# A hybrid decoder block: in-place stick-breaking scans, joint head transfers, and four more gates as a unit of seven products

## The chip, the cores and the metric

The kernel runs on one core of one Trainium2 chip. The metric is the device time of one launch in microseconds (us). TensorE (PE in the profile) does the matrix products, VectorE (DVE) and ScalarE (ACT) the elementwise work, GpSimd (POOL) and SyncE (SP) mostly issue DMA transfers, and POOL builds a mask now and then.

## The reference, cut to what matters

All is float32; there are 1024 tokens of width 1024, 256 memory tokens, 8 stick-breaking heads and 8 forgetting heads of 64, and 4 memory heads of 128. `w_in` projects the normed tokens to all queries, keys, values and to 3 x 1024 gate logits.

```python
def stick_breaking_attention(q, k, v):
    # A[t,s] = beta[t,s] * prod_{s<j<t}(1-beta[t,j]), strictly causal
    ...
        z = einsum('bhtd,bhsd->bhts', q, k) * scale
        strict = s_idx < t_idx
        log_rem = where(strict, log_sigmoid(-z), 0.0)
        after = cumsum(log_rem, axis=3, reverse=True) - log_rem
        w = where(strict, exp(log_sigmoid(z) + after), 0.0)
        out = einsum('bhts,bhsd->bhtd', w, v)
...
h = rmsnorm(x); proj = h @ w_in
o_sb  = stick_breaking_attention(sb_q, sb_k, sb_v)
o_fox = forgetting_attention(rmsnorm(fx_q), rmsnorm(fx_k), fx_v, log_f)   # causal softmax
o_mem = memory_attention(rmsnorm(m_q), rmsnorm(m_k), m_v)                 # softmax over 256
gates = sigmoid(gate_logit.reshape(b, s, 3, 1024))
merged = gates[0]*(o_sb @ w_branch_sb) + gates[1]*(o_fox @ w_branch_fox) + gates[2]*(o_mem @ w_branch_mem)
x = x + merged @ w_out
x = x + relu(rmsnorm(x) @ w_ff_up)**2 @ w_ff_down
```

## The kernel before, in words

**Precision.** A product of float32 matrices is three passes: both operands are split into a rounded part and the rest, and the passes are high by high, high by low, low by high (`passes`, `split` at L1052: ACT rounds at L1054, DVE subtracts at L1055).

**Units of seven products.** A matrix product whose two sides are cut into 2 x 2 blocks can be made from seven block products in place of eight (the kinds P1 to P7, in the order `KINDS`, L1354). `unit_products` (L1416, its matmuls are recorded on L1456) does so for the projections in `PROJ`: stick-breaking keys and queries, memory queries, forgetting keys and queries, stick-breaking values, and then the gate units of `GATES`, four gates of 128 columns each: `ga` holds gates 16 to 19, `gb` 20 to 23, `gc` 0 to 3. POOL brings the four weight blocks of a unit (L1373), DVE makes sums of them and `split` rounds them (`unit_prep`, L1379), PE multiplies, and DVE and ACT add up and evict (`unit_evict`, L1490; `unit_final`, L1519). These units run one after the other ahead of the attention. In it there are 24 gates: 0 to 7 belong to the stick-breaking branch, 8 to 15 to the forgetting branch, 16 to 23 to the memory branch.

**Dense gates.** Gates 4 to 7 and 10 to 13 are made by `dense_T` (L1147), one gate at a time: 8 steps of the contraction, 2 halves of 512 tokens, 3 passes, so 48 matmuls recorded on L1144. Gates 14 and 15 go together in `dense_two` (L1163), gate 9 comes earlier and gate 8 with the values. A gate's result goes through ACT into a row tile and by SP to `gate_scr` in device memory (`gate_put`, L1631). The three branch products follow in the order memory, stick-breaking, forgetting. The first two are `dense_branch(0)` and `dense_branch(1)` (L1728), 192 matmuls each, also on L1144; the last is `last_branch` (L1871), written out after the attention.

**Order.** The part up to `last_branch` is scheduled by a small planner at build time (`Machine`, L185 to 282). Each piece of work is a generator that asks for an engine (`Op`, with a cost from hand-written formulas), for a buffer (`Get`), or waits for an event. The planner plays this through with its own clock and emits the instructions in the order in which it began them. Gates and branch products are marked `side=True`: on PE they are chosen only when no attention operation is ready, so they fill the holes of the attention. `branches[0]` may begin only when all earlier dense tasks have been taken, `branches[1]` when `branches[0]` has been. Transfers are generators with a planned cost of their own (`transfer`, L296).

**Stick-breaking attention.** There are four pairs of heads `sb` and then four pairs `fox` (L809). For a head and 128 query rows, `sb_tile` (L812) goes over chunks of up to 512 keys, the last chunk first in the scan. The queries carry a sign such that `Sigmoid(+scale * sc)` is 1 - beta and `Sigmoid(-scale * sc)` is beta. Per chunk: two score matmuls (L823, L824); in the chunk that holds the diagonal, DVE adds a mask block of large numbers to PSUM (L834), so that 1 - beta is 1 and beta is 0 there; two ACT sigmoids, one into a tile `rho` taken from `RQ` (L827), one into the row tile `beta` (L828); and one DVE scan from right to left (L843) that leaves 1 - (what is left of the stick) in `beta`: `out = rho * out_before + beta`. `RQ` holds four 512-wide halves of two of the three row tiles of `RR`; `whole_again` (L1626) gives these two back after the four stick-breaking pairs. With the remaining one the memory attention works meanwhile (`RR`).

`unit` (L888) takes two such row tiles, transposes blocks of them on PE (L917), splits each turned block into a rounded part (ACT, L922) and the rest (DVE, L924), multiplies by the values (L934), and evicts. Since the row tile holds sums rather than weights, the values are differences of neighbouring rows (`value_step`, L1568).

**Loads of the heads.** `load_pairs` (L984) brings each head's operands from device memory by DMAs that POOL issues (`put`, L1004). `p_scr` holds for each projection two tensors, rounded part and rest. For each half of 512 tokens, `k1` is the rounded keys twice (lower and upper 64 partitions), `k2` the rest of the keys (twice for `sb`), `q` the rounded queries over the rest. That is 12 DMAs for a stick-breaking head, 16 for a forgetting head.

**Memory attention** (`memory`, L573, outputs at L701) runs within the stick-breaking stage, and its outputs are what `dense_branch(0)` multiplies. The forgetting attention (`fox_tile`, L854, scores on L869) follows, then the rest of the second branch, `last_branch`, the output projection (L1981) and the MLP (L2658).

Of the kernel before, what the change touches and what calls it, by code (L numbers as in the profile page):

```python
# [21 lines left out]
P = 128  # L22
# [5 lines left out]
HD = 64  # L28
# [15 lines left out]
def tile_hybrid_block(  # L44
# [58 lines left out]
    sm = C.p.tile([P, 8], F32, tag="sm", name="sm")  # L103
    zero, one = sm[:, 0:1], sm[:, 1:2]
    nc.vector.memset(zero, 0.0)
    nc.vector.memset(one, 1.0)
    gq2, gk2, gmq, gmk, bfg, eps = (sm[:, i:i + 1] for i in range(2, 8))
    nc.vector.memset(eps, EPS * 2.0 ** (2 / 3))

    def root_table():  # L110
# [8 lines left out]
    p_scr = {k: [dram.tile([512, S], F32, name=f"{k}_scr{i}", tag=f"{k}_scr{i}") for i in range(2)]  # L119
             for k in ("sbq", "sbk", "fxq", "fxk", "mq")}  # L120
# [230 lines left out]
    ES, OO, EL, RR, HT, PH, PL, OB, VV, BK, LATER, NONE, RQ = (Places([]) for _ in range(13))  # L351
# [221 lines left out]
    def memory():  # L573
        yield pairs[0].over

        def fetched_q(h, half):
            q = yield Get(HT, 2)

            def issue():
                for t, scr in zip(q, p_scr["mq"]):  # L580
                    nc.gpsimd.dma_start(f32(t), scr[h * P:(h + 1) * P, half * 512:(half + 1) * 512])
            yield from transfer(issue, 2 * P * 512 * 4, 1.1, queue_="POOL")
            q_of[h, half] = q
        q_of = {}
        for c in range(2):
            yield in_scr["mq", c]
            kv = yield Get(HT, 4)

            def issue():
                for i, t in enumerate(kv):  # L590
                    nc.gpsimd.dma_start(f32(t), m_scr[c][:, i, :])
            loaded = spawn(transfer(issue, 4 * P * 512 * 4, 2.2, queue_="POOL"), -20.0)
            evs = []
            for h in (2 * c, 2 * c + 1):
                for half in range(2):
                    ev = spawn(fetched_q(h, half), -300.0)
                    yield ev
                    yield loaded
                    if len(evs) > 1:
                        yield evs[-2]  # L600
                    evs.append(spawn(mem_attention(h, half, kv, q_of[h, half]), -10.0))
            if c:
                machine.fire(mem_in)
            for ev in evs:
                yield ev
            HT.put(*kv)
        machine.fire(mem_over)
# [204 lines left out]
    def sb_tile(pair, b, i, beta):  # L812
# [5 lines left out]
        def chunk(ci, c, m, u):  # L818
            rho = yield Get(RQ)
            sc = yield Get(SC)  # L820

            def scores():
                nc.tensor.matmul(sc[:, :m], q, pair.t["k1", b, ci][:, :m], start=True, stop=False)  # L823
                nc.tensor.matmul(sc[:, :m], q, pair.t["k2", b, ci][:, :m], start=False, stop=True)  # L824

            def sigmoids():
                nc.scalar.activation(rho[:, :u], sc[:, :u], AF.Sigmoid, scale=HD ** -0.5)  # L827
                nc.scalar.activation(beta[:, c:c + u], sc[:, :u], AF.Sigmoid, scale=-HD ** -0.5)  # L828
# [59 lines left out]
    def unit(pair, b, g, es):  # L888
# [5 lines left out]
        scr, r0 = o_scr[0 if pair.kind == "sb" else 1], (2 * pair.p + b) * HD  # L894
# [5 lines left out]
        def block(k):  # L900
# [11 lines left out]
            def turn():  # L912
# [71 lines left out]
    def load_pairs():  # L984
        yield ready
        for c, pair in enumerate(pairs):
# [5 lines left out]
            for b in range(2):  # L992
# [4 lines left out]
                def halves(half):  # L997
# [7 lines left out]
                    lower, upper, f4 = slice(0, HD), slice(HD, P), slice(HD, HD + 4)  # L1005

                    def keys():
                        put("k1", lower, ks_[0][rows, cols])
                        put("k1", upper, ks_[0][rows, cols])
                        put("k2", lower, ks_[1][rows, cols])  # L1010
                        if fox:
                            put("k2", f4, fk_scr[2 * p + b, :, cols])
                        else:
                            put("k2", upper, ks_[1][rows, cols])

                    def queries():
                        put("q", lower, qs[0][rows, cols])
                        put("q", upper, qs[1][rows, cols])
                        if fox:
                            put("q2", lower, qs[0][rows, cols])  # L1020
# [3 lines left out]
                evs = [spawn(transfer(k0_, 4 * HD * 2048, 1.6, queue_="POOL"), -20.0), spawn(transfer(k1_, 4 * HD * 2048, 1.6, queue_="POOL"), -20.0),  # L1024
                       spawn(transfer(q1_, (3 if fox else 2) * HD * 2048, 1.2, queue_="POOL"), -20.0),
                       spawn(transfer(q0_, (3 if fox else 2) * HD * 2048, 1.2, queue_="POOL"), -20.0)]
# [328 lines left out]
    GATES = {"ga": 16, "gb": 20, "gc": 0}  # L1355
# [163 lines left out]
    def unit_final(u, ct, q, src, of_bank=False):  # L1519
# [14 lines left out]
        elif u in ("sbq", "sbk"):  # L1534
# [10 lines left out]
            def out_():  # L1545
                for scr, t_ in zip(p_scr[u], (hi, lo)):
                    nc.sync.dma_start(scr[rows, cols], t_)
            spawn(counted(u, c, spawn(stored(out_, hi, lo))))
        else:
# [5 lines left out]
            def out_(hi, lo):  # L1555
                for scr, t_ in zip(p_scr[u], (hi, lo)):
# [4 lines left out]
    def masked(t):  # L1561
        nc.gpsimd.memset(t, 0.0)
        nc.gpsimd.affine_select(out=t[:, 384:], in_=t[:, 384:], pattern=[[-1, P + 1]], compare_op=ALU.is_ge,
                                fill=-NEG, base=0, channel_multiplier=1)
# [32 lines left out]
    def second_part():  # L1597
        def opened(name, *tags):
            pool = holder[name] = Pool(name, **{tag: n for _, tag, n, _, _ in tags})
            for place, tag, n, shape, dt in tags:  # L1600
# [6 lines left out]
               (LATER, "later", 1, 513, F32))  # L1607
        later = holder["later"] = LATER.free[0]
# [17 lines left out]
    def whole_again(tiles_):  # L1626
        for pair in pairs[:4]:
            yield pair.over
        RR.put(*tiles_)
# [1091 lines left out]
```

## Time and profile before

| | before |
|---|---|
| median of 3 runs | 1686.24 us (1685.2 to 1687.55) |
| span of the profiled execution | 1686.7 us |
| instructions in it | 25003 |
| DMA traffic | 284.32 MB, mean 169 GB/s |

The page of the profile has, in this order: the busy time of each engine with its share of the span and the count of instructions; the span in 40 equal slices; the DMA queues; the chain of work that ended last; the costliest groups of instructions; and the DMA issues. Two lines of the slices give the picture. Each digit is the busy share of a slice in tenths, 9 being 90% or more, and a slice is 42.2 us:

```profile
PE   9999999999999999999999999999999999999999
...
PEclk9999999999999999999999999999999999999999
```

In the lists of groups, "L1144 PE MATMUL sc<-h,whi 128x512" is the instruction that is recorded on line 1144, writing tile `sc` from the tiles `h` and `whi`; behind the bar stand the busy time and the mean time of one in ns, and then the idle time of the engine just ahead of them with what ended it. PEld is the loading of weights into PE, which overlaps its matmuls. Windows are given in us from the start of the span.

### The profile page before, as it was taken

To read this page: it belongs to the slowest core of one execution; us is meant where nothing else is said; L and a number is where in the kernel's file an instruction comes from. 1 tells how busy PE (TensorE), PEld (TensorE's weight loads), DVE (VectorE), ACT (ScalarE), POOL (GpSimd) and SP (SyncE) were. 2 spreads that over 40 slices of the span, in tenths; PEclk is the share of its full clock that TensorE was granted. 3 is DMA by queue.
4 is the path that set the end of the run, shared out by engine and by line. 5 is a ranking of instruction groups with operands and counts; after the bars stand their busy time and mean duration, and the time that the engine had idled before them with its cause. 6 is when DMAs were issued, how large, how long until landed. Compare 5 with 4: busy or idle time off the path is not lost.

```text
span 1686.7 us, 25003 instructions
## 1 busy us (share of the span) xinstructions
PE 1675.3 (99%) x9118; PEld 1432.0 (85%) x9118; DVE 1293.0 (77%) x2079; ACT 848.9 (50%) x1474; POOL 255.2 (15%) x440
## 2 busy tenths in 40 slices
PE   9999999999999999999999999999999999999999
PEld 9998899998888888888888887878888887888887
DVE  7977778855459888867877898987777776688775
ACT  6455555534358888866761446433333344332331
POOL 0000000000253151254400011022111120000000
PEclk9999999999999999999999999999999999999999
DMA  7445434467475365387747542144444484564532
GB/s 245 157 150 182 149 119 150 146 194 243 127 232 161 111 186 151 117 240 224 236 146 245 183 162 100 57 162 155 152 150 137 150 307 171 202 202 143 198 125 75
DMA packets 142221, 284.32 MB, mean 169 GB/s; under 512 B 16913, under 2 KB 53329, under 8 KB 142098
## 3 DMA queue, kind: packets, MB, share of 16 engines
q1 hardware_dynamic: 110562, 183.08, 32.0%
q0 software_dynamic: 31536, 99.64, 19.5%
q8 instruction: 72, 1.18, 0.3%
q14 instruction: 51, 0.42, 0.1%
HBM read 189.83 MB, written 92.83 MB: 168 GB/s over the span
## 4 chain that ended last, share of the span: by engine, by line
PE 92%; DVE 5%; DMA 2%; ACT 1%; issue 1%; SPq 0%; DVEq 0%; ACTq 0%
PE pp L1456 11%; PE pp L1144 10%; PE pp L1981 10%; PE pp L2658 8%; PE sc L1456 7%; PE sc L1144 6%; PE sc L1981 5%; PE sc L2658 4%; PE tr L2658 4%; PE tr L917 4%; PE pv L1456 3%; PE pv L2658 3%; PE tr L1981 2%; PE sc L934 2%; PE pp L934 2%; DVE h L1917 1%
## 5 line engine op out<-in xcount | busy, mean ns | idle before, releaser
L1055 DVE TENSOR_TENSOR wlo<-raw,whi 128x1024 fp32r<-128x1024 f32 (+1 forms) x88 | 107.5, 1222 | 80.2 <-ACT whi L1054 80.0
L1054 ACT ACTIVATE whi<-raw 128x1024 fp32r<-128x1024 f32 (+1 forms) x88 | 93.2, 1059 | 78.8 <-PE pp L1456 32.7
L2658 PE MATMUL pp<-h,sop 128*128 128x512 f32 x540 | 128.4, 396 | 0.0
L2658 PEld LDWEIGHTS pp<-h,sop 128*128 128x128 f32 x540 | 101.6, 188 | 24.4
L1981 PE MATMUL pp<-h,oh 128*128 128x512 f32 x384 | 121.1, 397 | 0.7 <-ACT cu L2066 0.6
L924 DVE TENSOR_TENSOR ptl<-tr,pth 128x512 fp32r<-128x512 f32 (+1 forms) x160 | 99.1, 628 | 24.1 <-ACT pth L922 23.1
L922 ACT ACTIVATE pth<-tr 128x512 fp32r<-128x512 f32 (+1 forms) x160 | 87.4, 556 | 36.0 <-PE sc L934 15.8
L1981 PEld LDWEIGHTS pp<-h,oh 128*128 128x128 f32 x384 | 72.0, 188 | 19.0 <-ACT cu L2066 1.4
L2573 ACT ACTIVATE h<-t 128x2048 fp32r<-128x2048 f32 (+1 forms) x17 | 30.7, 1814 | 110.2 <-DVE t L1917 97.4
L1373 POOL DMA_DIRECT2D raw<-w_in x32 | 24.2, 755 | 395.1 <-DVE wlo L1055 395.1
L1144 PE MATMUL sc<-h,whi 128*128 128x512 f32 (+1 forms) x254 | 77.7, 389 | 0.0
L1456 PE MATMUL pp<-h,whi 128*128 128x512 f32 x248 | 77.5, 394 | 0.0
L1981 PE MATMUL pp<-h,ol 128*128 128x512 f32 x192 | 76.1, 396 | 0.0
L1456 PE MATMUL pp<-whi,h 128*128 128x256 f32 x384 | 71.8, 283 | 0.0
L843 DVE TENSOR_TENSOR_SCAN e<-r,e 128x384 f32<-128x384 f32 (+3 forms) x64 | 66.3, 1044 | 6.9 <-ACT e L828 6.5
L1974 ACT ACTIVATE oh<-raw 128x512 fp32r<-128x512 f32 x64 | 39.4, 625 | 61.8 <-DVE raw L1917 61.8
L2658 PE MATMUL sc<-h,sop 128*128 128x512 f32 x264 | 63.7, 396 | 0.0
L2658 PE MATMUL tr<-h,sop 128*128 128x512 f32 x264 | 63.4, 396 | 0.0
L1917 DVE TENSOR_TENSOR sop<-ur,sop 128x2048 fp32r<-128x2048 f32 (+1 forms) x28 | 61.8, 2211 | 2.0 <-ACT sop L2586 2.0
L917 PE MATMUL tr<-ident,e 128*128 128x128 f32 x416 | 62.7, 273 | 0.0
L1456 PEld LDWEIGHTS pp<-whi,h 128*128 128x128 f32 x384 | 60.2, 188 | 0.0
L2658 PEld LDWEIGHTS sc<-h,sop 128*128 128x128 f32 x264 | 49.6, 188 | 12.3 <-DVE sop L1917 0.5
(558 smaller groups left out, 5087.7 us busy)
## 6 DMA issues: line engine op xcount, KB each, us to landing
ur<-s_scr SPq DMA_DIRECT2D x26, 1024.0 KB
raw<-w_in POOLq DMA_DIRECT2D x42, 512.0 KB, 4.9
raw<-w_up SPq DMA_DIRECT2D x60, 256.0 KB
s_scr<-s POOLq DMA_DIRECT2D x60, 256.0 KB, 2.7
g<-w_down SPq DMA_DIRECT2D x14, 1024.0 KB
s_scr<-cu POOLq DMA_DIRECT2D x48, 256.0 KB, 2.8
h<-sbk_scr POOLq DMA_DIRECT2D x64, 128.0 KB, 3.2
o<-gate_scr SPq DMA_DIRECT2D x32, 256.0 KB
```

The lines of the kernel that those rows point to most:

```text
L843: nc.vector.tensor_tensor_scan(out=back, data0=rho[:, :u][:, ::-1], data1=back, initial=0.0 if last else beta[:, c + u:c + u + 1], op0=ALU ...
L917: nc.tensor.transpose(tr[:, jj * 256 + a * P:jj * 256 + (a + 1) * P], es[a][:, j * P:(j + 1) * P], ident)
L922: yield Op("ACT", act_time(512 - lo_c), lambda: nc.scalar.activation(ph[:, lo_c:], tr[:, lo_c:], AF.Copy))
L924: yield Op("DVE", dve_time(512 - lo_c), lambda: nc.vector.tensor_tensor(pl[:, lo_c:], tr[:, lo_c:], f32(ph[:, lo_c:]), ALU.subtract))
L934: nc.tensor.matmul(pv[0][:, c_:256], pair.v[:, j, b, :], p_[:, jj * 256 + c_:(jj + 1) * 256], start=(k == 0 and n_ == 0 and i == 0), stop= ...
L1054: yield Op("ACT", 0.03 + act_time(m), lambda: nc.scalar.activation(hi, raw, AF.Copy))
L1055: yield Op("DVE", dve_time(m), lambda: nc.vector.tensor_tensor(lo, raw, f32(hi), ALU.subtract))
L1144: nc.tensor.matmul(ps, a_, b_, start=(first and i == 0), stop=(last and i == n - 1))
L1456: nc.tensor.matmul(out_, a_, b_, start=(first and n == 0 and j == 0), stop=(last and n == 3 and j == len(todo) - 1), skip_group_check=True)
L1917: nc.vector.tensor_tensor(out_, a_, b_, op)
L1981: nc.tensor.matmul(ps, w[a_][:, k * P:(k + 1) * P], h[b_][k], start=(first and k == 0 and i == 0), stop=(last and k == 3 and i == 2), skip ...
L2658: nc.tensor.matmul(ps, a_[:, c, qs], b_[:, c, :], start=(kind in ("P1", "P2", "P7") and c == 0 and i == 0), stop=(kind in ("P2", "P4", "P3 ...
```

## The change

It has four parts.

1. **What is left, in place.** `sb_tile` makes one sigmoid, 1 - beta, into the row tile and scans it in place: `out = max(in * out_before, floor)`, beginning with 1. In the chunk with the diagonal, `floor` is a tile that holds 1.0 on the masked places and 0 elsewhere, so that the masked part stays at 1; in the other chunks it is a broadcast zero. The row tile then holds what is left of the stick, and the eviction of a turned block subtracts 1 (a bias of -1 in ACT's copy, a -1 in DVE's subtraction). The sign of the value differences is turned. The addition of the mask to PSUM, the second sigmoid and the `RQ` tiles go. The floor takes half of one lent row tile, so that one tile of `RR` is lent and not two.
2. **Joint transfers.** `p_scr` becomes one tensor with a leading 2. `k1`, and `k2` of the stick-breaking heads, come by one DMA whose source is broadcast twice; `q` by one DMA over both parts. A stick-breaking head takes 6 DMAs, a forgetting head 12. The planner's costs for issuing them are changed to match.
3. **Gates 4 to 7** become a fourth gate unit `gd`, made after `gc` and ahead of the attention; the list of dense gates leaves them out by itself.
4. The mask `later` of the forgetting attention is 512 wide and not 513; it and `floor` are made by `masked` with a fill and a base.

```diff
+    sm = C.p.tile([P, 9], F32, tag="sm", name="sm")
+    zero, one, minus = sm[:, 0:1], sm[:, 1:2], sm[:, 8:9]
...
-    p_scr = {k: [dram.tile([512, S], F32, name=f"{k}_scr{i}", tag=f"{k}_scr{i}") for i in range(2)]
+    p_scr = {k: dram.tile([2, 512, S], F32, name=f"{k}_scr", tag=f"{k}_scr") for k in ("sbq", "sbk", "fxq", "fxk", "mq")}
...
-    def sb_tile(pair, b, i, beta):
+    def sb_tile(pair, b, i, left):
...
         def chunk(ci, c, m, u):
-            rho = yield Get(RQ)
             sc = yield Get(SC)
+            part = left[:, c:c + u]
...
             yield Op("PE", 2 * mm_time(max(m, 256)), scores)
+            yield Op("ACT", act_time(u), lambda: nc.scalar.activation(
+                part, sc[:, :u], AF.Sigmoid, scale=HD ** -0.5), table=AF.Sigmoid)
+            SC.put(sc)
             last = c + u == n
-            if last:
-                dg = sc[:, u - P:u]
-                yield Op("DVE", 0.22, lambda: nc.vector.tensor_tensor(
-                    dg, dg, holder["later"][:, 385:513], ALU.add))
-            yield Op("ACT", act_time(u, u), sigmoids, table=AF.Sigmoid)
-            SC.put(sc)
             if not last:
                 yield scanned
-
-            def scan():
-                back = beta[:, c:c + u][:, ::-1]
-                nc.vector.tensor_tensor_scan(out=back, data0=rho[:, :u][:, ::-1], data1=back,
-                                             initial=0.0 if last else beta[:, c + u:c + u + 1],
-                                             op0=ALU.mult, op1=ALU.add)
-            yield Op("DVE", 0.1 + 0.00215 * u, scan, 0.14)
-            RQ.put(rho)
+            back = part[:, ::-1]
+            floor = holder["floor"][:, 512 - u:512] if last else zero.to_broadcast([P, u])
+            yield Op("DVE", 0.1 + 0.00215 * u, lambda: nc.vector.tensor_tensor_scan(
+                out=back, data0=back, data1=floor[:, ::-1], initial=1.0 if last else left[:, c + u:c + u + 1],
+                op0=ALU.mult, op1=ALU.max), 0.14)
...
-            yield Op("ACT", act_time(512 - lo_c), lambda: nc.scalar.activation(ph[:, lo_c:], tr[:, lo_c:], AF.Copy))
+            h_, t_ = ph[:, lo_c:], tr[:, lo_c:]
+            yield Op("ACT", act_time(512 - lo_c), lambda: nc.scalar.activation(
+                h_, t_, AF.Identity, bias=minus) if of_sb else nc.scalar.activation(h_, t_, AF.Copy))
             pl = yield Get(PL)
-            yield Op("DVE", dve_time(512 - lo_c), lambda: nc.vector.tensor_tensor(
-                pl[:, lo_c:], tr[:, lo_c:], f32(ph[:, lo_c:]), ALU.subtract))
+            yield Op("DVE", dve_time(512 - lo_c), lambda: nc.vector.scalar_tensor_tensor(
+                pl[:, lo_c:], t_, -1.0, f32(h_), ALU.add, ALU.subtract) if of_sb else nc.vector.tensor_tensor(
+                pl[:, lo_c:], t_, f32(h_), ALU.subtract))
...
+                    def twice(k, src):
+                        nc.gpsimd.dma_start(f32(t[k]), src)
...
                     def keys():
-                        put("k1", lower, ks_[0][rows, cols])
-                        put("k1", upper, ks_[0][rows, cols])
-                        put("k2", lower, ks_[1][rows, cols])
+                        high, low = (ks_[i, rows, cols] for i in range(2))
+                        twice("k1", high.unsqueeze(0).to_broadcast([2, HD, 512]))
                         if fox:
+                            put("k2", lower, low)
                             put("k2", f4, fk_scr[2 * p + b, :, cols])
                         else:
-                            put("k2", upper, ks_[1][rows, cols])
+                            twice("k2", low.unsqueeze(0).to_broadcast([2, HD, 512]))
...
                     def queries():
-                        put("q", lower, qs[0][rows, cols])
-                        put("q", upper, qs[1][rows, cols])
+                        twice("q", qs[:, rows, cols])
...
-    GATES = {"ga": 16, "gb": 20, "gc": 0}
+    GATES = {"ga": 16, "gb": 20, "gc": 0, "gd": 4}
...
-        yield Op("DVE", dve_time(512), lambda: nc.vector.tensor_tensor(a, a, b, ALU.subtract))
+        yield Op("DVE", dve_time(512), lambda: nc.vector.tensor_tensor(a, b, a, ALU.subtract))
...
-        halves = [RR.free.popleft() for _ in range(2)]
-        RQ.put(*(t[:, i * 512:(i + 1) * 512] for t in halves for i in range(2)))
-        spawn(whole_again(halves))
-        yield Op("POOL", 1.0, lambda: masked(later))
+        lent_ = RR.free.popleft()
+        holder["floor"] = lent_[:, :512]
+        spawn(whole_again(lent_))
+        yield Op("POOL", 1.0, lambda: masked(holder["floor"], 1.0, -1))
+        yield Op("POOL", 1.0, lambda: masked(holder["later"], -NEG, 0))
```

More of the change, by code (lines that the diff above doesn't have):

```diff
@@ L102, in tile_hybrid_block @@
     make_identity(nc, ident)
-    sm = C.p.tile([P, 8], F32, tag="sm", name="sm")
-    zero, one = sm[:, 0:1], sm[:, 1:2]
+    sm = C.p.tile([P, 9], F32, tag="sm", name="sm")
+    zero, one, minus = sm[:, 0:1], sm[:, 1:2], sm[:, 8:9]
     nc.vector.memset(zero, 0.0)
     nc.vector.memset(one, 1.0)
+    nc.vector.memset(minus, -1.0)
     gq2, gk2, gmq, gmk, bfg, eps = (sm[:, i:i + 1] for i in range(2, 8))
@@ L350, in tile_hybrid_block @@
     PP, SC, TR, PV = (banks(tag) for tag in ("pp", "sc", "tr", "pv"))
-    ES, OO, EL, RR, HT, PH, PL, OB, VV, BK, LATER, NONE, RQ = (Places([]) for _ in range(13))
+    ES, OO, EL, RR, HT, PH, PL, OB, VV, BK, LATER, NONE = (Places([]) for _ in range(12))
     SN, RS, S1 = tiles(E, "sn", 10, 512), tiles(R, "raw", 4, 1024), R.t("s1", [P, 4, 256])
@@ L1023, in load_pairs @@
                 (k1_, q1_), (k0_, q0_) = halves(1), halves(0)
-                evs = [spawn(transfer(k0_, 4 * HD * 2048, 1.6, queue_="POOL"), -20.0), spawn(transfer(k1_, 4 * HD * 2048, 1.6, queue_="POOL"), -20.0),
-                       spawn(transfer(q1_, (3 if fox else 2) * HD * 2048, 1.2, queue_="POOL"), -20.0),
-                       spawn(transfer(q0_, (3 if fox else 2) * HD * 2048, 1.2, queue_="POOL"), -20.0)]
+                evs = [*(spawn(transfer(k_, 4 * HD * 2048, 1.5 if fox else 1.0, queue_="POOL"), -20.0) for k_ in (k0_, k1_)),
+                       *(spawn(transfer(q_, (3 if fox else 2) * HD * 2048, 1.5 if fox else 0.5, queue_="POOL"), -20.0) for q_ in (q1_, q0_))]
                 if b == 0:
@@ L1545, in out_ @@
             def out_():
-                for scr, t_ in zip(p_scr[u], (hi, lo)):
+                for scr, t_ in zip((p_scr[u][0], p_scr[u][1]), (hi, lo)):
                     nc.sync.dma_start(scr[rows, cols], t_)
```

29 lines of the change are left out of this document (13 added, 16 removed).

## The prediction, written before the change was measured

> **What bounds the kernel now.** I read the page first: the busy row, the slices, the chain of waits.
>
> ```profile
> span 1686.7 us, 25003 instructions
> ...
> PE 1675.3 (99%) x9118; PEld 1432.0 (85%) x9118; DVE 1293.0 (77%) x2079; ACT 848.9 (50%) x1474; POOL 255.2 (15%) x440
> ...
> PE 92%; DVE 5%; DMA 2%; ACT 1%; issue 1%; SPq 0%; DVEq 0%; ACTq 0%
> ```
>
> PE is busy for 99% of the span and holds 92% of the chain. A busy PE need not be a PE at its peak, since its ends are modelled, so I went on to the stages and counted matmuls. The first answer below is the busy time by stage: the window and its length, then busy us and instructions of PE, PEld, DVE, ACT and POOL, the granted clock, the DMA share and GB/s. The second is the same for L1144 alone, the dense matmuls (gates and branch products), the third for L1456, the units of seven products.
>
> ```profile
> 400.20:439.20 39.00, 39.00 (x170) 31.57 (x168) 21.91 (x30) 17.83 (x29) 4.72 (x7) 1.00 0.68 215
> ...
> 478.00:718.00 240.00, 240.00 (x1474) 211.05 (x1473) 204.22 (x377) 202.03 (x445) 75.28 (x136) 1.00 0.52 156
> 718.00:878.00 160.00, 158.53 (x1024) 140.22 (x1024) 122.02 (x324) 111.75 (x258) 61.93 (x114) 0.99 0.71 213
> 878.00:923.00 45.00, 45.00 (x197) 36.52 (x196) 34.91 (x49) 9.43 (x15) 2.24 (x3) 1.00 0.70 221
> ```
> ```profile
> 478.00:718.00 240.00, 132.19 (x480) 85.35 (x480) 1.00 0.52 156
> 718.00:878.00 160.00, 68.92 (x240) 42.71 (x241) 0.99 0.71 213
> 878.00:923.00 45.00, 44.70 (x192) 35.87 (x192) 1.00 0.70 221
> ```
> ```profile
> 400.20:439.20 39.00, 39.00 (x170) 31.57 (x168) 1.00 0.68 215
> ```
>
> A dense 512-column matmul takes 44.70 / 192 = 0.233 us; less the tail of the last one, 0.232. A gate unit is 7 x 2 x 4 x 3 = 168 of them, 39.0 us. From 478 to 718 us runs the stick-breaking attention with the memory attention (the first stage), from 718 to 878 the forgetting attention (the second). In both, attention goes first on PE and dense matmuls fill the holes. The L1144 counts say how much: 480 + 240, less 48 products of the memory attention (8 x 2 x 3), is 672 = ten gates of 48 and the 192 of the first branch. The third row's 192 are the second branch, which ran alone after attention had ended. So PE is the bound, attention has 44.5 us of dense work left behind it, and a change is worth what it takes from PE, if the filling lasts.
>
> **The change, part by part.**
>
> *The fourth unit.* Gates 4 to 7 leave the filling: 4 x 48 = 192 matmuls, 192 x 0.232 = 44.5 us. The unit adds 168 x 0.232 = 39.0 us ahead of attention. PE gains 24 x 0.232 = 5.6 us; no other part of the change touches PE's work. The unit's sums, splits and evictions lie under its matmuls: in the unit of the first fence DVE was busy for 21.91 and ACT for 17.83 us of 39.00 while PE never stopped. Were that cover gone, each us that DVE exceeds 39 would be one of PE's. POOL brings the unit's four blocks there (4.72 us busy) and is rid of four gate loads in attention; the gates' eight stores move to the same place on SP, where the DMA engines stand at 0.68 of their time in that row. The bytes are the same.
>
> *Stick-breaking.* Removed: the 64 mask additions in PSUM (L834) and 96 second sigmoids (L828). The 96 scans (L843) and the 80 rounding pairs keep their counts.
>
> ```profile
> 478.00:718.00 240.00, 18.15 (x64) 1.00 0.52 156
> ```
> ```profile
> 478.00:718.00 240.00, 48.39 (x96) 1.00 0.52 156
> ```
> ```profile
> 478.00:718.00 240.00, 10.85 (x9) 1.00 0.52 156
> ```
> ```profile
> L738 ACT ACTIVATE sn<-tr,sm 128x512 fp32r<-128x512 f32 x26 | 17.5, 684 | 10.8 <-PE tr L732 10.4
> L473 ACT ACTIVATE h<-tr 128x512 fp32r<-128x512 f32 x8 | 4.6, 592 | 3.3 <-DVE st L368 1.7 <-PE tr L465 1.6
> ```
> ```profile
> L474 DVE TENSOR_TENSOR h<-tr,h 128x512 fp32r<-128x512 f32 x8 | 5.4, 687 | 0.7 <-ACT h L473 0.6
> ...
> L1539 DVE SCALAR_TENSOR_TENSOR sn<-pp,sn 128x512 fp32r<-128x512 f32 x2 | 1.4, 692 | 0.8 <-ACT sn L1538 0.7
> ```
>
> These rows are DVE on L834, ACT on L828 and DVE on L1055 (weight splits) in the first stage, then two ACT groups and two DVE groups that price the new forms. DVE loses 18.2 us, and 3 of its 9 weight splits at 10.85 / 9 = 1.2, so 3.6: 204.2 goes to 182.4. The subtraction with a -1 in it costs 692 against 687 ns, nothing. ACT loses 48.4 and the evictions of three gates, 6 x 0.592 = 3.6 (their weight roundings, not priced here, would be more); it gains the pointer bias, 684 - 592 = 92 ns on 80 copies, 7.4: 202.0 goes to 157. A scan with MAX for ADD, in place and with a stride-0 second input, is not in this stage; the nearest row is the scan here, and I take no difference (a gain has no reason; 96 x 0.05 = 5 us more is the other end).
>
> What is this worth? Only the length W of the first stage, 240 us now, and that only through the filling. PE's attention work there is 240 less 435 x 0.232 = 101, so 139 us (3 of the memory's products come later); the second stage takes 55 of filling in 160 us, 0.35 per us. Before attention ends the new filling without the second branch is six gates and the first branch, 480 x 0.232 = 111 us; wanted are (W - 139) + 55, 156 at W = 240. The second branch can help only once its operands are split:
>
> ```profile
> 846.84 0.69 DVE L1055 TENSOR_TENSOR h<-r,h 128x512 fp32r<-128x512 f32 x1 [0.40 <-ACT h L1054]
> ...
> 855.09 0.69 DVE L1055 TENSOR_TENSOR h<-r,h 128x512 fp32r<-128x512 f32 x1
> ```
>
> That was 855, 23 us before attention's end, so it gives 23 x 0.35 = 8. PE stays fed if W is at most 240 - 44.5 + 8 = 204; every us above is one of idle PE. This is the cover on which the 5.6 us rest.
>
> W is between two ends. Ahead of the memory attention the stage runs at DVE's limit:
>
> ```profile
> 500.00:520.00 20.00, 20.00 (x127) 17.58 (x126) 19.00 (x32) 16.21 (x37) 7.13 (x13) 1.00 0.69 190
> 520.00:540.00 20.00, 20.00 (x127) 17.64 (x126) 19.14 (x33) 17.00 (x40) 6.31 (x12) 1.00 0.42 135
> ...
> 740.00:760.00 20.00, 18.53 (x105) 15.50 (x104) 14.20 (x44) 14.63 (x32) 8.50 (x17) 0.91 0.66 210
> ```
>
> DVE is busy 38.14 of 40, 0.953: 182.4 / 0.953 = 191. At the stage's mean share, 204.2 / 240 = 0.85, it is 214. I take 200: nearer to the first, since ACT, at 0.84 of the stage the other limit, falls to 157 / 200 = 0.79, the chain of a chunk loses two steps, and the memory attention gets a second row tile. At 200 PE is not short.
>
> *Joint transfers.* 96 + 128 = 224 issues become 48 + 96 = 144; at 0.53 us (25.4 / 48 below) POOL saves 42 us, off the path.
>
> ```profile
> L1004 POOL DMA_DIRECT2D h<-fxq_scr x48 | 25.4, 539 | 6.0 <-DMA h<-fxk_scr 5.3 <-issue 0.6
> ```
> ```profile
> h<-fxq_scr POOLq DMA_DIRECT2D x48, 128.0 KB, 4.0
> ```
> ```profile
> q0 software_dynamic: 31536, 99.64, 19.5%
> ```
> ```profile
> 694.70 0.54 POOL L1004 DMA_DIRECT2D h<-fq_scr  x1
> ...
> 705.70 0.40 PE L869 MATMUL pp<-h,h 128*128 128x512 f32 x1
> ```
>
> By this row (packets, MB, share of 16 engines) the bytes of POOL's queue cost 0.195 x 1686.7 x 16 / 99640 KB = 0.053 us per KB of one engine, so 256 KB over 16 engines take 0.8 us: as now. The cover in the tightest place that I found: the queries issued last at 694.7 are used at 705.7, 11 us, of which 4.0 are the landing; 7 are left. The Trainium skill, DMA: Bandwidth & Descriptors, Rules for kernel authors, says that an outermost dimension smaller than 16, a leading broadcast of c copies for instance, confines a DMA to c engines. No row here shows such a shape.
>
> The new mask tile is one fill more on POOL, busy for 4.72 of 39.00 us in a gate unit; nothing. Sum: -5.6 us. The profiled execution's span is 1686.7, the median of the runs 1686.24, so I carry the difference over: 1686.24 - 5.6 = **1680.6 us**. What a measurement can tell from no change here is about 0.2%, 3.4 us.
>
> **The rivals.**
>
> *The filling runs out* (slower). The place is the hand-over from the last gate to the first branch, which waits for the memory attention. It is tight already:
>
> ```profile
> 718.51 0.60 ACT L701 ACTIVATE o<-pp 128x512 f32<-128x512 f32 x1
> ```
> ```profile
> 742.59 0.50 PE L869 MATMUL pv<-h,h 128*128 128x512 f32 x1 [1.47 <-DVE st L874]
> ```
>
> Memory's last output came at 718.5, the first branch matmuls at 740, and PE, with no dense work left in front of a score tile, stood for 1.47 us. Six gates are 66.8 us. If memory still ends with the stage and branch work 22 us later, the want is (W - 139) + 22 x 0.35, so PE idles W - 198: 16 us at 214, 1680.6 + 16 = 1696.6. It ends slower from W = 207 on (9 us); with memory done earlier, by the bound of 204, from 213 on. For it: the mean share of 0.85, and that two memory tasks at a time hold more PSUM banks. Against: ACT's relief. Idle can cost more than itself: in the row of 740:760 the granted clock is 0.91, 0.09 x 20 = 1.8 us on top of 1.47, so 16 us in such gaps could be 35, 1715. The Trainium skill, TensorE: Matmul & The Clock Gate, HAM section, halves the clock after an idle window of 3.4 us until a busy one has passed. By that rule gaps of 1.5 us would cost nothing more and the 16 us stay 16, 1696.6; the trace agrees with its amount (half the clock for 3.4 us is 1.7 lost, the row has 1.8), not with the length of its idle window.
>
> *A part of it* (no change): an idle of 2 to 9 us, which is W of 200 to 207 with memory late or 206 to 213 with memory early; say 4, 1684.6. For it: W's two ends lie on both sides. Against: with memory early, my 200 has 4 us to spare.
>
> *Transfers on two engines* (slower): 256 KB x 0.053 / 2 = 6.8 us instead of 0.8, so landing 6 us later; the cover of 7 hides it. Where the cover is shorter by 3 us in, say, four of the 16 head loads, PE waits 12: 1692.6. Against: the cover, and that nothing here shows such a split. By the rule cited above this is what the chip would do, with the covers left to decide.
>
> *It doesn't do what it says*: the copy with a bias might need another function table than the sigmoid.
>
> ```profile
> L647 ACT ACT_TABLE_LOAD x8 | 10.3, 1283 | 0.1
> ```
>
> This is a group of the first stage. Two loads of 1.28 us for each of the 80 would be 205 us of ACT, so W at 362 and 1680.6 + 158 = 1839. Nothing for it: the plain copy in the same place brings none.
>
> **How the numbers follow.** Forecast 0.59, filling runs out 0.16, a part of it 0.20, two engines 0.04, tables 0.01. Faster by over 0.2% is the forecast, 0.59; within, 0.20; slower, 0.21. The forecast's own range is 1677 (the 1.47 us and its 1.8 of clock gone: 1677.3) to 1682.8. The range goes up to 1692, an idle of 11 us, and leaves out most of the two slow cases; down it ends at 1677.
>
> **What would show it.** Right: 192 fewer matmuls on L1144 (960 of 512 columns are ten gates, gate 9, two branches and memory's 48; 768 then) and 168 more on L1456; the first stage at about 200 us, DVE near 0.93 and ACT below 0.8 in it; L1144 alone for over 30 us after attention; no PE wait above 2 us between the stages. Wrong: a first stage of over 207 us, gaps on PE with a clock below 1 near the end of the gates or late in the second stage, PE waiting at L823 or L869 for a head's transfer, or table loads around L922.

## The result: 56 us slower, and the profile after

The changed kernel took 1742.85 us (median of four), the kernel before 1685.9 us. One of the four took 3345.15 us, which nothing here explains; without it the median is 1741.71 us (1738.69 to 1743.98), and that is the figure that the differences below are taken from. The ratio, without it too, is 1.0328, 95% interval 1.0314 to 1.0342. The profiled execution took 1738.69 us.

From the page of the changed kernel: the span, the busy row, the chain of waits, and POOL's queue (packets, MB, share of 16 engines).

```profile
span 1736.9 us, 24656 instructions
...
PE 1690.3 (97%) x9094; PEld 1435.1 (83%) x9094; DVE 1291.2 (74%) x2029; ACT 820.5 (47%) x1381; POOL 239.5 (14%) x362
...
q0 software_dynamic: 66096, 99.92, 21.1%
...
PE 83%; DMA 5%; DVE 5%; ACT 3%; issue 1%; POOL 0%; SPq 0%; ACTq 0%; POOLq 0%; DVEq 0%
```

PE still looks busy, at 97%, but it has fallen from 92% to 83% of the chain, and DMA has gone from 2% to 5%. The queue moves nearly the same bytes in twice the packets. By stage (window, length, then PE, PEld, DVE, ACT and POOL busy, clock, DMA share, GB/s); at 911 the attention's last blocks had been turned:

```profile
517.00:717.00 200.00, 191.67 (x1196) 168.57 (x1194) 165.73 (x256) 142.36 (x278) 60.40 (x84) 0.98 0.69 169
717.00:810.00 93.00, 76.50 (x518) 64.22 (x517) 66.14 (x188) 66.28 (x172) 35.37 (x57) 0.97 0.58 153
810.00:911.00 101.00, 88.69 (x528) 76.55 (x527) 70.03 (x182) 59.47 (x137) 22.91 (x35) 0.93 0.75 190
911.00:971.00 60.00, 60.00 (x265) 48.79 (x264) 40.00 (x56) 11.30 (x17) 3.00 (x4) 1.00 0.62 189
```

In the first three rows PE stands still for 8.3, 16.5 and 12.3 us, 37 together, where the attention of the kernel before had 1.5. The granted clock is 2%, 3% and 7% short, which costs 14 us at most, since part of it falls while PE stands anyway. By the busy row PE stood for 46.6 us of the whole span, 35.2 more than before, and its matmuls took 15.0 us longer although 5.6 us of them are gone; together these are the 50.2 us by which the span grew. How much of the longer matmuls is the clock stays open. The last row is dense work that attention left behind: 60 us where there were 48 (875 to 923).

The hand-over from the gates to the first branch is in the timeline (start, length, engine, line): ACT's eviction of the last gate, ACT's last output of the memory attention, and PE's first matmul of the first branch.

```profile
694.60 0.60 ACT L1632 ACTIVATE o<-sc 128x512 f32<-128x512 f32 x1 [0.66 <-PE sc L1138]
```
```profile
793.03 0.59 ACT L701 ACTIVATE o<-pv 128x512 f32<-128x512 f32 x1
```
```profile
809.44 0.73 PE L1138 MATMUL pp<-whi,whi 128*128 128x512 f32 x1
```

For 115 us PE had no gate and no branch matmul, only the memory attention's own. The stick-breaking stage itself went fast: from its first score at 523.9 to the first forgetting score at 712.2 are 188 us (222 before, 483.4 to 705.7). But the memory attention, which had ended 13 us after that point, now ended 81 us after it.

### The profile page after: what moved, and what is told of

It is laid out like the page before. It is cut to its first block, busy times and chain, and to the rows that moved or that the text cites. A ratio compares the mean times of both kernels' runs of the same rounds, so it can differ in the third digit from the quotient of the medians.

```text
span 1736.9 us, 24656 instructions
## 1 busy us (share of the span) xinstructions
PE 1690.3 (97%) x9094; PEld 1435.1 (83%) x9094; DVE 1291.2 (74%) x2029; ACT 820.5 (47%) x1381; POOL 239.5 (14%) x362
## 3 DMA queue, kind: packets, MB, share of 16 engines
q0 software_dynamic: 66096, 99.92, 21.1%
## 4 chain that ended last, share of the span: by engine, by line
PE 83%; DMA 5%; DVE 5%; ACT 3%; issue 1%; POOL 0%; SPq 0%; ACTq 0%; POOLq 0%; DVEq 0%
PE pp L1450 11%; PE pp L1976 10%; PE sc L1450 8%; PE pp L2653 8%; PE pp L1138 7%; PE sc L1976 5%; PE sc L2653 4%; PE tr L2653 4%; PE sc L1138 4%; PE pv L1450 3%; PE pv L2653 3%; PE tr L907 2%; PE tr L1976 2%; PE pv L927 1%; PE pp L927 1%
## 5 line engine op out<-in xcount | busy, mean ns | idle before, releaser
L1450 PE MATMUL pp<-h,whi 128*128 128x512 f32 x296 | 92.7, 394 | 0.0
L907 PE MATMUL tr<-ident,e 128*128 128x128 f32 x416 | 66.2, 282 | 17.9 <-DVE ptl L916 8.6
L907 PEld LDWEIGHTS tr<-ident,e 128*128 128x128 f32 x416 | 49.6, 144 | 31.1 <-DVE ptl L916 11.1
L1450 PEld LDWEIGHTS pp<-h,whi 128*128 128x128 f32 x296 | 55.6, 188 | 12.9
L917 DVE TENSOR_TENSOR ptl<-tr,pth 128x384 fp32r<-128x384 f32 (+1 forms) x80 | 50.3, 634 | 19.2 <-ACT pth L914 18.8
L1138 PE MATMUL pp<-h,whi 128*128 128x512 f32 x198 | 63.8, 403 | 0.0
L913 ACT ACTIVATE pth<-tr,sm 128x384 fp32r<-128x384 f32 (+1 forms) x80 | 50.4, 646 | 24.7 <-PE pp L927 12.6
## 6 DMA issues: line engine op xcount, KB each, us to landing
h<-sbk_scr POOLq DMA_DIRECT2D x32, 256.0 KB, 12.1
```

What stands on the lines that cost most here:

```text
L907: nc.tensor.transpose(tr[:, jj * 256 + a * P:jj * 256 + (a + 1) * P], es[a][:, j * P:(j + 1) * P], ident)
L917: pl[:, lo_c:], t_, -1.0, f32(h_), ALU.add, ALU.subtract) if of_sb else nc.vector.tensor_tensor(
L1138: nc.tensor.matmul(ps, a_, b_, start=(first and i == 0), stop=(last and i == n - 1))
L1450: nc.tensor.matmul(out_, a_, b_, start=(first and n == 0 and j == 0), stop=(last and n == 3 and j == len(todo) - 1), skip_group_check=True)
```

## The experiments

Theory A: gates 4 to 7 are missing in the filling, and the first branch waits for the memory attention, so PE has no dense work. Theory B: PE waits because the joint transfers land late. The first four kernels undo one part of the change, or do one part alone.

**e1_split**, the changed kernel with the transfers of before:

```diff
-                        twice("k1", high.unsqueeze(0).to_broadcast([2, HD, 512]))
+                        put("k1", lower, ks_[0][rows, cols])
+                        put("k1", upper, ks_[0][rows, cols])
...
-                        twice("q", qs[:, rows, cols])
+                        put("q", lower, qs[0][rows, cols])
+                        put("q", upper, qs[1][rows, cols])
```

> The changed kernel with the separate transfers of before for the heads' operands (224 issues, 128 rows never in one), all else as changed. Theory A (the filling runs out: gates 4 to 7 are gone from it, and the first branch waits for the memory attention, which ends 75 us into the second stage): the idle PE between the last gate and the first branch stays, about 30 us of the 56, so 1712 to 1725 us. Theory B (transfers on two engines: PE waits because a joint transfer lands 12 us after its issue in place of 3): 1680 to 1690 us, the forecast of the rest.

Measured: 1716.11 us, 1.0173 of before (1.0157 to 1.0188). The transfers cost 25.6 us, and some 30 are left without them: both theories hold, for about half of the loss each. The edit also puts back the planner's costs for issuing the transfers, so the order of the instructions changes with them; no run separates the two.

**e2_nogd**, the changed kernel without the fourth unit:

```diff
-    GATES = {"ga": 16, "gb": 20, "gc": 0, "gd": 4}
+    GATES = {"ga": 16, "gb": 20, "gc": 0}
```

> The changed kernel without the fourth gate unit: gates 4 to 7 are dense again and fill the attention; joint transfers and the in-place scans stay. Theory A: the filling lasts about as before, and only what the transfers cost is left, 1690 to 1710 us. Theory B: the unit saves 5.6 us and nothing else, so its loss makes it 1745 to 1750 us.

Measured: 1715.95 us, 1.0166 (1.0147 to 1.0185), outside both ranges. The unit costs 25.8 us, as A says, but the transfers cost 27 (beside e5_stick below) with all the filling there, more than A allowed.

**e3_before_gd**, the kernel before with the fourth unit alone:

```diff
-    GATES = {"ga": 16, "gb": 20, "gc": 0}
+    GATES = {"ga": 16, "gb": 20, "gc": 0, "gd": 4}
```

> The kernel before with the fourth gate unit alone. Theory A: gates run out some 45 us before the memory attention ends, and PE idles for most of what the attention leaves free until then, 1712 to 1730 us. Theory B: the unit is worth its 24 matmuls, 1680 to 1681 us.

Measured: 1721.52 us, 1.0212 (1.0195 to 1.023). By itself the unit costs 35 us. The attention, from the first score to the last turned block, took 386.5 us here (522.2 to 908.7) and 363.8 in e1_split (524.5 to 888.3). Both ran short of filling, so the difference, 23 us, is what the in-place scans take from the attention's own length, together with the second row tile that they leave to the memory attention.

**e4_before_joint**, the kernel before with the joint transfers alone (the edit of e1_split the other way round):

> The kernel before with the joint transfers alone. Theory A: late landings are mostly hidden while dense work is there to fill, 1686 to 1700 us. Theory B: they cost nearly all that the change lost, 1720 to 1745 us. In both a joint transfer lands 8 us or more after its issue, where a separate one took 3 to 4.

Measured: 1715.68 us, 1.0186 (1.0156 to 1.0216), between the two ranges: dense work does not hide late landings. (By the medians the stick-breaking heads' transfers landed after 12.1 and 13.7 us.) Why, its timeline shows; first POOL's issues, then ACT, then PE:

```profile
494.11 1.61 POOL L1006 DMA_DIRECT2D h<-sbq_scr  x2
...
496.59 0.92 POOL L1062 DMA_DIRECT2D raw<-w_in  x1
```
```profile
515.83 1.06 ACT L1054 ACTIVATE whi<-raw 128x1024 fp32r<-128x1024 f32 x1 [5.69 <-DMA raw<-w_in]
516.79 0.26 ACT L826 ACTIVATE r<-pv 128x128 f32<-128x128 f32 x1
516.95 0.27 ACT L827 ACTIVATE e<-pv 128x128 f32<-128x128 f32 x1
```
```profile
512.64 0.28 PE L933 MATMUL pp<-ptl,v 128*128 128x256 f32 x1
517.27 0.58 PE L822 MATMUL pv<-h,h 128*128 128x256 f32 x1 [4.35 <-ACT e L827]
```

A gate's weights were issued at 496.59, behind joint transfers on the same queue, and were there at about 515.8, after 19 us. ACT stood for 5.69 us at rounding them, with the attention's sigmoids behind it in its order, so no score tile came free and PE stood for 4.35. No head's transfer was late at this place. The same happened once more: ACT stood for 5.88 us until 623.5 at weights issued at 606.8, and PE then for 3.30 (of which ACT spent 1.28 on loading a function table). ACT's waits for DMAs over the attention, those of over 3 us (us in total, times, longest), first before, then e4_before_joint:

```profile
ACT h L1054 <- DMA r<-o_scr: 5.9, 5, 3.6
```
```profile
ACT whi L1054 <- DMA raw<-w_in: 11.6, 2, 5.9
ACT h L1054 <- DMA r<-o_scr: 8.4, 4, 3.9
ACT whi L1054 <- DMA r<-o_scr: 3.8, 1, 3.8
ACT whi L1054 <- DMA raw<-w_b: 3.4, 1, 3.4
```

**e5_stick**, the in-place scans alone (the edits of e1_split and e2_nogd together):

> The in-place scans alone: the changed kernel with separate transfers and with gates 4 to 7 dense, as before. Theory A (PE is the bound wherever dense work is at hand, so less work on DVE and ACT gives nothing by itself): 1684 to 1690 us, with the attention ending about 20 us earlier and the branch work behind it longer by as much. Rival: the new scan chain is itself slower, as the rest of the sum (1743 less 27 for the unit and 27 for the transfers) could mean: 1689 us or more.

Measured: 1688.51 us, 1.0015 (1.0006 to 1.0023), within 0.2% of before, as A says; whether the 2.5 us are the new chain or the order that came out of it stays open. Of A's second half less came true: the attention ended at 867.8, not 20 but 7 us earlier than before (874.9). The windows say why. They are cut at the last stick-breaking score and at the attention's end, first before, then e5_stick:

```profile
482.00:704.00 222.00, 222.00 (x1375) 195.70 (x1374) 191.48 (x338) 190.01 (x424) 71.09 (x127) 1.00 0.53 157
704.00:875.00 171.00, 169.53 (x1088) 149.70 (x1087) 131.90 (x358) 121.40 (x276) 63.51 (x117) 0.99 0.69 205
```
```profile
482.00:664.00 182.00, 182.00 (x1137) 160.46 (x1136) 155.81 (x235) 137.94 (x269) 64.96 (x118) 1.00 0.55 169
664.00:868.00 204.00, 204.00 (x1307) 180.89 (x1307) 153.11 (x397) 142.77 (x331) 68.91 (x126) 1.00 0.66 189
```

The first stage has shrunk by 40 us and the second has grown by 33. The second half of the memory attention (outputs from 692 to 725; before, from 664 to 718, three of the four ahead of the cut) has moved from the one into the other and taken DVE work along, 153.11 us now against 131.90. And the second stage does not run at the first one's pace: DVE is 0.75 busy there (0.77 before), and 0.86 in the first, in both kernels.

Put on one after the other, the parts cost 2.5 us for the scans (e5_stick), 27.6 for the unit (e1_split less e5_stick) and 25.6 for the transfers (the changed kernel less e1_split). That these make up the whole 55.7 is so by construction. That the prices hold elsewhere is what the other runs say: the transfers cost 27.4 without the unit (e2_nogd less e5_stick) and 29.3 in the kernel before; the unit costs 25.8 beside the joint transfers, but 35 without the scans.

**e6_swap**, e1_split with the stick-breaking branch ahead of the memory branch:

```diff
-    order = ((2, 2), (0, 0), (1, 1))
+    order = ((0, 0), (2, 2), (1, 1))
...
-        yield mem_over
+        for pair_ in pairs[:4]:
+            yield pair_.over
```

> The changed kernel with separate transfers (1716 us before this edit) and the stick-breaking branch ahead of the memory branch, whose operands are there some 75 us earlier. Theory A (the idle PE comes from the first branch's wait for the memory attention): the gap from the last gate to the first branch falls from 107 us to about 45, and two thirds of the idle with it, 1692 to 1700 us. Rival (there is too little dense work for the attention, whatever its order): 1712 to 1718 us.

Measured: 1698.97 us, 1.0075 (1.0061 to 1.0088), as A says: 17 of the unit's 27.6 us are back. The gap from the last gate to the first branch, first in e1_split, then in e6_swap:

```profile
698.00:800.00 102.00, 87.30 (x586) 74.67 (x587) 77.41 (x211) 76.76 (x188) 41.16 (x78) 0.97 0.51 153
```
```profile
698.00:734.00 36.00, 29.44 (x187) 24.85 (x186) 28.62 (x76) 28.34 (x57) 11.52 (x23) 0.95 0.55 173
734.00:894.00 160.00, 159.47 (x1030) 140.64 (x1030) 131.19 (x338) 112.79 (x276) 56.64 (x104) 1.00 0.71 209
```

PE stands for 6.6 us in place of 14.7, and as soon as branch work is there, it hardly stands at all (0.5 us in 160).

**e7_contig**, e5_stick with one transfer of 128 rows for the stick-breaking queries:

```diff
+    hq_scr = dram.tile([8, P, S], F32, name="hq_scr", tag="hq_scr")
...
-                        put("q", lower, qs[0][rows, cols])
-                        put("q", upper, qs[1][rows, cols])
+                        nc.gpsimd.dma_start(f32(t["q"]), hq_scr[2 * p + b, :, cols])
```

> The in-place scans alone, and the stick-breaking queries by one transfer of 128 rows from a store that keeps rounded part and rest of a head together, so that the source's outermost dimension is 128 and not 2 (the store takes four DMAs in place of two). If the leading 2 makes the joint transfers slow: the 16 query loads land after 3 to 5 us, without the packets of 8 bytes, and the time is that of the scans alone. If it is their size of 256 KB or being one transfer: 10 us or more, as in the changed kernel.

Measured: 1688.67 us, 1.0018 (1.0008 to 1.0027), that of e5_stick. Median us from issue to landing, in the changed kernel and then here:

```profile
h<-sbk_scr POOLq DMA_DIRECT2D x32, 256.0 KB, 12.1
...
h<-sbq_scr POOLq DMA_DIRECT2D x16, 256.0 KB, 13.6
```
```profile
h<-sbk_scr POOLq DMA_DIRECT2D x64, 128.0 KB, 3.0
...
h<-hq_scr POOLq DMA_DIRECT2D x16, 256.0 KB, 4.1
```

The same 256 KB in one transfer land after 4.1 us when the source's outermost dimension is 128, and after 13.6 when it is 2. Part of the 13.6 can be the wait behind the keys' joint transfers, which are separate here. But the size and being one transfer are ruled out, so it is the leading 2. The broadcast keys were not tried in another form.

**e8_onerow**, e5_stick with two row tiles lent, so that one is left to the memory attention:

> The in-place scans alone, with two row tiles lent as before, so that the memory attention has one and works on one task at a time. If the second row tile is what keeps the memory attention up with the shorter stage: its last output comes later, and the time is 5 to 12 us above the scans alone. If two tasks at a time get in each other's way: the same time or less.

Measured: 1694.15 us, 1.0048 (1.0034 to 1.0061), 5.6 us above e5_stick; the last memory output comes at 765.9 in place of 725.0. The second row tile helps; that two tasks at a time hold each other up is refuted.

**e9_gate9**, e6_swap with gate 9 left to the filling:

```diff
-    h_tasks += [dense_gate(9), *kv_tasks]
+    h_tasks += [*kv_tasks]
...
-    gates = [dense_gate(n, may_gate) for n in (*range(16, 24), *range(0, 8), *range(10, 14)) ...
+    gates = [dense_gate(n, may_gate) for n in (*range(16, 24), *range(0, 8), *range(9, 14)) ...
```

> The changed kernel with separate transfers and the stick-breaking branch first (1699 us before this edit), and gate 9 no longer made ahead of the units but left to the filling: 48 matmuls, 11.1 us, move from ahead of the attention into it. Theory A (what is still missing there is dense work while the attention runs, some 13 us): most of the 11 us come back, 1688 to 1693 us. Rival (what is left is another cost, of the swap or of the fourth unit): 1697 to 1700 us.

Measured: 1694.12 us, 1.0052 (1.0035 to 1.0069), outside both ranges: 4.9 of the 11 us are back, less than half. More filling helps, but it did not last either: the branch came at 730.2, 15 us after the last gate's eviction at 715.5. That is still 5.6 us above the scans alone, so the unit's saving was not reached.

**e10_kvearly**, e1_split with the memory attention's second keys and values brought early:

```diff
+            if c == 0:
+                fetch_kv(1, (yield Get(HT, 4)))
...
-            for ev in evs:
-                yield ev
-            HT.put(*kv)
+            all_.append(spawn(kv_back(evs, kv)))
```

> The changed kernel with separate transfers (1716 us before this edit), the memory branch first as in the changed kernel, and the memory attention's second keys and values brought ahead of its first tasks, with the second half's tasks following the first half's without waiting for all of them. If the 18 us between the fourth memory output and the second keys' transfer are what makes the memory attention late: it ends 20 to 40 us earlier, and PE loses about a third of that less, 1703 to 1710 us. Rival (the memory attention is late for its late start and its pace beside a faster stick-breaking attention): no gain, 1714 to 1718 us.

Measured: 1712.48 us, 1.0154 (1.0139 to 1.0169). The issue of the second keys moved, first e1_split, then this one:

```profile
715.60 2.12 POOL L591 DMA_DIRECT2D h<-m_scr  x4
```
```profile
611.65 2.13 POOL L594 DMA_DIRECT2D h<-m_scr  x4
```

The memory attention ended at 748.3 in place of 789.2, 41 us earlier, and the time fell by 3.6 us only, which neither side had said: the attention's last turned block came at 898.8, 10 us later than in e1_split. That the same work was only done in another order is a reading, not shown. No version here is faster than the kernel before.

## Why the prediction was wrong, point by point

**Right: what PE and the new instructions cost.** The window from 480 to 971 us has x720 on L1138, which with gate 9's 48, made earlier, is the 768 forecast. The new forms cost what was said; DVE in the changed kernel, then ACT:

```profile
L834 DVE TENSOR_TENSOR_SCAN e<-e,sm 128x512 f32<-128x512 f32 x32 | 40.5, 1267 | 0.5
...
L916 DVE SCALAR_TENSOR_TENSOR ptl<-tr,pth 128x512 fp32r<-128x512 f32 x48 | 32.1, 677 | 8.8 <-ACT pth L913 8.6
```
```profile
L913 ACT ACTIVATE pth<-tr,sm 128x512 fp32r<-128x512 f32 x48 | 32.9, 689 | 16.0 <-PE pp L927 11.3 <-PE pv L927 3.3 <-DVE ptl L916 1.0
L914 ACT ACTIVATE pth<-tr 128x512 fp32r<-128x512 f32 x48 | 28.2, 591 | 12.7 <-PE pp L927 9.2 <-PE pv L927 3.4
```

The pointer bias is 98 ns (92 forecast). The scan with MAX takes 1267 ns (1264 before) and the subtraction with -1 677 (682 before), so they cost nothing. The copies brought no table loads.

**Wrong: "At 200 PE is not short".** The stage of stick-breaking did shrink, to 188 us in the changed kernel, below the 204 up to which the prediction held PE to be fed. What failed is that bound, and with it the idle time at the hand-over, which stood in the sum as nothing. The prediction let the memory attention end with the stage, 22 us ahead of branch work at worst, and gave the second stage its old 160 us. On the chip half of the memory attention went over into the second stage: the branch came 97 us after the first forgetting score (712.2 to 809.4), and in e5_stick the second stage grew by 33 us while the first shrank by 40. What the scans really took from the attention was 23 us (e1_split beside e3_before_gd), where the prediction took 40. So the rival "the filling runs out" was the mechanism, in the place that it named, but not on its condition: it asked for a first stage of over 207 us. Its price can be read from the busy rows of e5_stick and then e1_split:

```profile
PE 1676.0 (99%) x9118; PEld 1431.8 (85%) x9118; DVE 1279.4 (76%) x2016; ACT 817.8 (48%) x1374; POOL 257.0 (15%) x442
```
```profile
PE 1685.5 (98%) x9094; PEld 1432.6 (84%) x9094; DVE 1291.3 (75%) x2029; ACT 820.9 (48%) x1381; POOL 256.2 (15%) x442
```

In spans of 1686.6 and 1714.4 us, PE stood for 18.3 us more in e1_split, and its matmuls took 15.1 us longer than 24 fewer of them should: 33 us, for 27.6 lost and 5.6 not saved. The rival had said 16 us of standing and at most 35 with a low clock. The size fits by luck: its 16 belonged to a first stage of 214 us and a wait of 22 for branch work, and in e1_split these were 183 and 92. e6_swap shows what that wait is worth: with another branch first, 17 us come back. Part of the rest is the missing amount of dense work, of which e9_gate9 brings 4.9 back; the last 5.6 us above the scans alone stay open.

**Wrong: "the cover of 7 hides it".** The joint transfers stood in the sum as nothing and cost 25.6 us. The trace bears out the rival's two engines and nearly their price: by the medians a joint transfer of the stick-breaking heads lands 9 to 10 us later than a separate one before, one of the forgetting heads 5 to 7, 6 forecast. In the records of single packets, the 64 packets of 4096 bytes of the first joint transfer start in pairs, two at a time, until other transfers join; those of separate transfers run up to 16 and more at a time. What failed is that only the heads' own loads were looked at. In e4_before_joint weights on POOL's queue, with less cover, came late as well, and ACT stood at them with the attention behind it; that is shown at two places, with 4.35 and 3.30 us of PE's time. In the changed kernel the late transfers that ACT and DVE stood at were mostly others:

```profile
ACT h L1048 <- DMA r<-o_scr: 11.3, 3, 4.7
ACT o L701 <- DMA gate_scr<-o: 6.1, 1, 6.1
ACT whi L1048 <- DMA r<-o_scr: 5.2, 1, 5.2
ACT whi L1048 <- DMA raw<-w_in: 2.6, 1, 2.6
```
```profile
DVE r L1670 <- DMA r<-l_scr: 4.6, 1, 4.6
```

All but the weights `raw` are on SP's queue, not POOL's, and PE's three longest waits, 5.6, 5.1 and 3.8 us, stand right behind those of 6.1, 5.2 and 4.6. But e1_split, with separate transfers, also has 3.6 us at `gate_scr` and 4.4 at `r<-o_scr`. So which part of the 25.6 us came by which queue stays open.

**The two rivals were priced one at a time.** Each got a chance as if the other were not there. Both came, and their costs add up: without the unit the transfers cost 27.4 us, with it 25.6.

**The clock.** The prediction had two prices for gaps. One was the row of before, where 1.47 us of waiting went with 1.8 us of clock. The other was the rule of the Trainium skill (TensorE: Matmul & The Clock Gate, HAM section) that only an idle window of 3.4 us halves it. Five windows of the changed kernel, then one of e1_split:

```profile
700.00:720.00 20.00, 13.58 (x85) 12.38 (x85) 14.07 (x32) 13.38 (x23) 4.98 (x9) 0.83 0.42 109
720.00:740.00 20.00, 16.94 (x118) 14.22 (x117) 15.61 (x47) 15.94 (x42) 4.13 (x8) 1.00 0.47 155
...
760.00:780.00 20.00, 16.88 (x114) 14.09 (x112) 16.15 (x50) 14.75 (x40) 6.95 (x11) 1.00 0.64 183
...
800.00:820.00 20.00, 10.85 (x46) 8.03 (x44) 5.41 (x9) 5.79 (x12) 6.55 (x11) 0.66 0.96 233
840.00:860.00 20.00, 16.19 (x97) 14.16 (x96) 12.85 (x37) 12.39 (x29) 6.47 (x10) 0.91 0.97 225
```
```profile
760.00:780.00 20.00, 18.03 (x117) 15.56 (x115) 14.98 (x43) 14.67 (x41) 8.27 (x16) 0.91 0.43 120
```

From 720 to 740 and from 760 to 780 of the changed kernel PE stood for 3 us each, in pieces of at most 1.2, and the clock stayed at 1.00. It fell where single waits were long: 5.6 us near 700, 5.1 near 803 and 3.3 near 811, 3.8 near 850. So far the rule agrees better than the row of before. But in the row of e1_split, where PE stood for 2 us with no wait above 1.1, the clock is 0.91, as it was before with 1.47. So here short gaps mostly cost only themselves, with two exceptions that stay unexplained. The long waits came with 1.8 to 6.8 us of lost clock in their window, and what of it falls while PE stands costs nothing: from 811.0 to 814.4 PE stood at a clock of 0.50.

## What to carry to other kernels

Where one engine is the bound and filling work keeps it fed, ask of every piece of filling when it becomes available, not only how much there is: a faster stage moves the work that gates the next filling, and that work keeps a pace of its own. A cheaper form of work that is taken out of the filling is paid for with idle time when the filling was just enough: the unit saved 5.6 us of matmuls and left the kernel 27.6 us slower all the same. A DMA whose source has an outermost dimension of 2 was slow here (12 to 14 us for 256 KB) and could hold up transfers behind it (a gate's weights took 19 us), so its price is looked for at all engines that wait for a transfer, and not only at its own consumer. Storing the data so that one dimension of 128 leads took the price away for the queries (4.1 us).

## What the runs showed of the hardware beyond that

Each of the 80 joint transfers brought 448 packets of 8 bytes with it (35,840 in the attention's part of the trace, none in the kernel before), which is why, with 1,280 packets of 4 bytes fewer, POOL's queue went from 31,536 to 66,096 packets at nearly the same bytes. One such packet took 9 ns by the median, against some 180 ns for one of 4096 bytes. Issuing a joint transfer took POOL 0.81 us where a separate one took 0.53, so 80 in place of 160 saved 20 us of issuing and not the 42 of the prediction, off the path in both.
